# A very short load on a second DMA queue, issued beside the first load, in a 3D average pooling kernel

## The chip, the cores and the metric

One core of one Trainium2 chip. The metric is device time in microseconds (us), as the median of several executions; lower is better.

## The reference, cut to what matters

```python
# x: (8, 32, 32, 32, 32) float32, kernel_size 2
# result: (8, 32, 16, 16, 16) float32
for i in range(16):
    for j in range(16):
        for k in range(16):
            window = x[:, :, 2*i:2*i+2, 2*j:2*j+2, 2*k:2*k+2]
            result[:, :, i, j, k] = np.mean(window, axis=(-3, -2, -1))
```

33.55 MB are read and 4.19 MB written. Every output is the sum of eight inputs times 0.125, so there is little to compute per byte.

## The kernel before: the parts that matter

The 256 pairs of batch and channel make two groups of 128 partitions. The input comes in eight pieces of 4 MB, each of 128 rows of 32 KB, through five buffers; the last two pieces are loaded as two halves each. VectorE adds three times per piece: over d, w and h. An engine (here SP or ScalarE) issues a load or store on its own queue; the 16 DMA engines then move it in packets, one row each for the loads here, and each engine ends its share with a 4-byte completion packet that counts up a semaphore (16 such packets per load in the trace). The transfer has landed when all 16 have counted.

```python
    plan = [
        (0, 0, (32,)), (0, 32, (32,)), (0, 64, (32,)), (0, 96, (32,)),
        (1, 0, (32,)), (1, 32, (32,)), (1, 64, (16, 16)), (1, 96, (16, 16)),
    ]
    # ... pool_unit: three VectorE instructions per part ...
    for t, k0, parts in plan:
        tin = pool_in.tile([P, 32 * KF], F32, tag="tin", name="tin")   # 5 buffers
        # ... per part kb:
            nc.sync.dma_start(out=v, in_=xv[...])                      # SP's queue
        # ... pool_unit on each part
    for queue, t, k0, kb in [(nc.scalar, 1, 0, 2), (nc.sync, 0, 0, 16),
                             (nc.sync, 1, 2, 12), (nc.sync, 1, 14, 2)]:
        queue.dma_start(out=ov[...], in_=obuf[t][...])                 # the four stores
```

The kernel is already tuned at its ends. The program begins with a block in which all engines meet at a barrier; the first load is moved ahead of SP's part of that barrier, so that it is issued with the program's first instruction:

```python
    load = next(i for i in program if isinstance(i, mybir.InstDMACopy))
    # ...
    program.remove(load)
    opening.insert(barrier, load)
```

Of the kernel before, what the change touches and what calls it, by code (L numbers as in the profile page):

```python
# [1 line left out]

# [4 lines left out]

F32 = mybir.dt.float32
KF = 256


@with_exitstack
def pool_rows(
    ctx: ExitStack,
    tc: tile.TileContext,
    x: bass.AP,
    kernel_size: int,
    out: bass.AP,
):
    nc = tc.nc  # L20
    assert kernel_size == 2, "only kernel_size == 2 supported"

    B, C, D, H, W = x.shape
    P = nc.NUM_PARTITIONS
    assert (B * C, D, H, W) == (2 * P, 32, 32, 32)
    add = mybir.AluOpType.add



    xv = x.rearrange("b c d h w -> (b c) (d h w)")  # L30
    ov = out.rearrange("b c d h w -> (b c) (d h w)")




    pool_in = ctx.enter_context(tc.tile_pool(name="pin", bufs=5))
    pool_out = ctx.enter_context(tc.tile_pool(name="pout", bufs=1))
    obuf = [pool_out.tile([P, 16 * KF], F32, name=f"obuf{t}") for t in range(2)]
    dummy = pool_out.tile([P, 1], F32, name="dummy")


    plan = [
        (0, 0, (32,)),
        (0, 32, (32,)),
        (0, 64, (32,)),
        (0, 96, (32,)),
        (1, 0, (32,)),
        (1, 32, (32,)),
        (1, 64, (16, 16)),
        (1, 96, (16, 16)),  # L50
    ]

    def pool_unit(buf, t, k0, kb):

        od = kb // 8
        a = buf.rearrange("p (o dd e) -> p o dd e", o=od, dd=2)
        b = buf[:, :od * 1024]
        nc.vector.tensor_add(  # L58
            out=b.rearrange("p (o e) -> p o e", o=od), in0=a[:, :, 0], in1=a[:, :, 1])
        bv = b.rearrange("p (e ww) -> p e ww", ww=2)  # L60
        c = buf[:, od * 1024:od * 1536]
        nc.vector.tensor_add(out=c, in0=bv[:, :, 0], in1=bv[:, :, 1])  # L62
        cv = c.rearrange("p (j hh k) -> p j hh k", hh=2, k=16)
        o0 = k0 * KF // 8
        nc.vector.tensor_tensor_reduce(  # L65
            out=obuf[t][:, o0:o0 + od * 256].rearrange("p (j k) -> p j k", k=16),
            in0=cv[:, :, 0], in1=cv[:, :, 1],
            scale=0.125, scalar=0.0, op0=add, op1=add, accum_out=dummy[:, :],
        )

    for t, k0, parts in plan:
        tin = pool_in.tile([P, 32 * KF], F32, tag="tin", name="tin")
        views = []
        o = 0
        for kb in parts:
            v = tin[:, o * KF:(o + kb) * KF]
            nc.sync.dma_start(  # L77
                out=v, in_=xv[t * P:(t + 1) * P, (k0 + o) * KF:(k0 + o + kb) * KF])
            views.append((v, k0 + o, kb))
            o += kb  # L80
        for v, k, kb in views:
            pool_unit(v, t, k, kb)



    for queue, t, k0, kb in [
        (nc.scalar, 1, 0, 2),
        (nc.sync, 0, 0, 16),
        (nc.sync, 1, 2, 12),
        (nc.sync, 1, 14, 2),  # L90
    ]:
        queue.dma_start(
            out=ov[t * P:(t + 1) * P, k0 * KF:(k0 + kb) * KF],
            in_=obuf[t][:, k0 * KF:(k0 + kb) * KF],
        )


def kernel(tc: tile.TileContext, x: bass.AP, kernel_size: int, out: bass.AP):
    nc = tc.nc
    pool_rows(tc, x, kernel_size, out)  # L100
    tc.close()
    tc.compile()  # L102
    blocks = nc.main_func.blocks



    opening, program = blocks[0].instructions, blocks[tc.starting_block_idx].instructions
    load = next(i for i in program if isinstance(i, mybir.InstDMACopy))
    assert load.engine == nc.sync.engine
    barrier = next(  # L110
        n for n, i in enumerate(opening)
        if i.engine == load.engine and isinstance(i, mybir.InstDrain))
    program.remove(load)
    opening.insert(barrier, load)




    closing = blocks[-1].instructions
    stores = [  # L120
        i for i in program
        if isinstance(i, mybir.InstDMACopy) and "out_" in i.outs[0].memref]
    kept = [u.id for i in stores for u in i.sync_info.on_update]
    kept = [n for j, n in enumerate(kept) if n not in kept[j + 1:]]
    final = next(
        i for i in closing
        if i.engine == nc.sync.engine and isinstance(i, mybir.InstDrain))
    waits = {w.id: w for w in final.sync_info.on_wait}
    closing[closing.index(final)] = mybir.InstDrain(
        name=final.name, engine=final.engine, ins=[], outs=[], is_reset_sema=False,  # L130
        sync_info=mybir.SyncInfo(
            on_wait=[w for n, w in waits.items() if n not in kept], on_update=[]))


    reset = next(
        n for n, i in enumerate(closing)
        if isinstance(i, mybir.InstDrain) and i.is_reset_sema)
    first, stop = closing[reset].reset_range_start, closing[reset].reset_range_stop
    assert isinstance(closing[reset + 1], mybir.InstISA)
    while len(closing) > reset:  # L140
        closing.pop()
    n = first
    while n < stop:
        m = n
        while m < stop and m not in kept:
            m += 1
        if m > n:
            closing.append(mybir.InstDrain(
                name=nc.get_next_instruction_name(), engine=nc.gpsimd.engine, ins=[], outs=[],
                is_reset_sema=True, reset_range_start=n, reset_range_stop=m))  # L150
            nc.gpsimd.sem_clear(range(n, m))
        n = m + 1
    for n in kept:
        w = waits[n]
        closing.append(mybir.InstEventSemaphore(
            name=nc.get_next_instruction_name(), engine=nc.sync.engine, ins=[], outs=[],
            sync_info=mybir.SyncInfo(
                on_wait=[w],
                on_update=[mybir.SyncUpdate(
                    sync_type="semaphore", id=n, ant_name=w.ant_name,  # L160
                    update_mode="sem-sub-imm", update_value=w.wait_value)])))


# [1 line left out]
_INS = ['x', 'kernel_size']  # L165
_OUTS = [((8, 32, 16, 16, 16), 'float32')]

_NUMBERS = {'kernel_size': 2}


# [26 lines left out]
```

## Time and profile before

| | before |
|---|---|
| median of the three runs | 91.57 us (91.52 to 91.82) |
| profiled execution, first to last instruction | 86.6 us |
| VectorE busy | 64.1 us, 74% |
| DMA | 421 GB/s mean over the span |

From the list of waits (columns: engine, line, who was waited for, total us, times, longest us):

```profile
DVE tin L58 <- DMA tin<-in_x_dram: 20.6, 6, 12.1
```

(DVE is VectorE; in the lines below ACT is ScalarE, and SPq and ACTq are the issuing sides of SP and ScalarE.) VectorE waits for nothing but loads: 12.1 us for the first and 1.7 us for each of the next five. The 12.1 us are the target of the change.

### The profile page before, as it was taken

How to read it: one execution, taken by the hardware profiler on the slowest of the kernel's cores; microseconds unless marked ns; L12 is line 12 of the kernel's file. 1: busy time of each engine (PE TensorE's matmuls, PEld its weight loads, DVE VectorE, ACT ScalarE, POOL GpSimd, SP SyncE). 2: the span in 40 equal slices, each digit the busy share in tenths (PEclk: the TensorE clock that was granted, in tenths of full speed). 3: DMA queues.
4: the chain of work that ended last, by engine and by line, in shares of the span. 5: the costliest groups of instructions: out<-in, count | busy, mean ns of one | idle time of the engine just before them, and what ended most of it. 6: DMA issues, size and time to landing. Idle time of an engine off the chain costs nothing.

```text
span 86.6 us, 91 instructions
## 1 busy us (share of the span) xinstructions
DVE 64.1 (74%) x40; POOL 0.2 (0%) x4
## 2 busy tenths in 40 slices
DVE  0000049993999749992999749992999999999994
POOL 0000000000000000000000000000000000000000
DMA  8889998899979999799988999699999999999999
GB/s 242 379 363 469 485 485 348 379 485 485 469 333 409 485 485 424 318 469 485 485 348 379 485 485 469 288 454 416 405 407 424 407 462 394 462 394 454 394 454 398
DMA packets 1774, 36.48 MB, mean 421 GB/s; under 512 B 192, under 2 KB 192, under 8 KB 320
## 3 DMA queue, kind: packets, MB, share of 16 engines
q1 hardware_dynamic: 1630, 36.22, 98.4%
q10 hardware_dynamic: 144, 0.26, 0.8%
HBM read 33.55 MB, written 4.19 MB: 436 GB/s over the span
## 4 chain that ended last, share of the span: by engine, by line
DMA 83%; DVE 14%; SPq 1%; issue 0%; DVEq 0%
DMA tin<-in_x_dram 83%; DVE tin L58 8%; DVE tin L62 4%; DVE obuf L65 2%; SPq L77 1%; DVE dummy L65 0%; DVEq L102 0%
## 5 line engine op out<-in xcount | busy, mean ns | idle before, releaser
L58 DVE TENSOR_TENSOR tin<-tin 128x4096 f32<-128x4096 f32 (+1 forms) x10 | 35.7, 3570 | 20.7 <-DMA tin<-in_x_dram 20.6
L62 DVE TENSOR_TENSOR tin<-tin 128x2048 f32<-128x2048 f32 (+1 forms) x10 | 18.6, 1865 | 0.3
L65 DVE CUSTOM_DVE_ANT_1 obuf<-tin 128x1024 f32<-128x1024 f32 (+1 forms) x10 | 10.1, 1011 | 0.3
L65 DVE DVE_READ_ACCUMULATOR2_ANT dummy<- 128x1 f32 x10 | 0.8, 82 | 0.0
L178 POOL MEMSET const-uint8-127<- 128x1 uint8 x1 | 0.1, 102 | 0.0
L178 POOL MEMSET const-bfloat16-1.0<- 128x1 bf16 x1 | 0.1, 101 | 0.0
L178 POOL MEMSET const-float32-0.0<- 128x1 f32 x1 | 0.1, 98 | 0.2 <-issue 0.2
L178 POOL MEMSET const-float32-1.0<- 128x1 f32 x1 | 0.1, 98 | 0.0
## 6 DMA issues: line engine op xcount, KB each, us to landing
tin<-in_x_dram SPq DMA_DIRECT2D x6, 4096.0 KB, 35.0
tin<-in_x_dram SPq DMA_DIRECT2D x4, 2048.0 KB, 38.9
out_dram<-obuf SPq DMA_DIRECT2D x1, 2048.0 KB, 36.8
out_dram<-obuf SPq DMA_DIRECT2D x1, 1536.0 KB, 8.8
out_dram<-obuf ACTq DMA_DIRECT2D x1, 256.0 KB, 9.9
out_dram<-obuf SPq DMA_DIRECT2D x1, 256.0 KB, 4.9
```

The costliest lines, as they stand in the source:

```text
L58: nc.vector.tensor_add(out=b.rearrange("p (o e) -> p o e", o=od), in0=a[:, :, 0], in1=a[:, :, 1])
L62: nc.vector.tensor_add(out=c, in0=bv[:, :, 0], in1=bv[:, :, 1])
L65: nc.vector.tensor_tensor_reduce(out=obuf[t][:, o0:o0 + od * 256].rearrange("p (j k) -> p j k", k=16), in0=cv[:, :, 0], in1=cv[:, :, 1], s ...
L77: nc.sync.dma_start(out=v, in_=xv[t * P:(t + 1) * P, (k0 + o) * KF:(k0 + o + kb) * KF])
L178: nc = _bacc.Bacc("TRN2", target_bir_lowering=False, num_devices=1)
```

## The change

The intent, as far as the code tells it: the first transfer of a program may have to wake something on its way, so a tiny one is sent beside it, on the other queue, to wake it first. Nobody reads what it brings.

```diff
     dummy = pool_out.tile([P, 1], F32, name="dummy")
+    first = pool_out.tile([16, 128], F32, name="first")
+    nc.scalar.dma_start(out=first[:, :], in_=xv[:16, :128])
...
-    load = next(i for i in program if isinstance(i, mybir.InstDMACopy))
-    assert load.engine == nc.sync.engine
-    barrier = next(...)
-    program.remove(load)
-    opening.insert(barrier, load)
+    loads = [i for i in program if isinstance(i, mybir.InstDMACopy)][:2]
+    # ... (an assert: the first fills `first`, the second `tin`)
+    for load in loads:
+        assert not load.sync_info.on_wait
+        barrier = next(...)          # the drain of the load's own engine
+        program.remove(load)
+        opening.insert(barrier, load)
```

More of the change, by code (lines that the diff above doesn't have):

```diff
@@ L107 @@
     opening, program = blocks[0].instructions, blocks[tc.starting_block_idx].instructions
-    load = next(i for i in program if isinstance(i, mybir.InstDMACopy))
-    assert load.engine == nc.sync.engine
-    barrier = next(
-        n for n, i in enumerate(opening)
-        if i.engine == load.engine and isinstance(i, mybir.InstDrain))
-    program.remove(load)
-    opening.insert(barrier, load)
+    loads = [i for i in program if isinstance(i, mybir.InstDMACopy)][:2]
+    assert [i.outs[0].bass_ap.tensor.name.split("_")[0] for i in loads] == ["first", "tin"]
+    for load in loads:
+        assert not load.sync_info.on_wait
+        barrier = next(
+            n for n, i in enumerate(opening)
+            if i.engine == load.engine and isinstance(i, mybir.InstDrain))
+        program.remove(load)
+        opening.insert(barrier, load)
     closing = blocks[-1].instructions
```

## The prediction

> **What bounds the kernel now.** I read the page from the top. First the engines, the DMA row in 40 slices, the queues and the memory traffic:
>
> ```profile
> DVE 64.1 (74%) x40; POOL 0.2 (0%) x4
> ...
> DMA  8889998899979999799988999699999999999999
> ...
> q1 hardware_dynamic: 1630, 36.22, 98.4%
> q10 hardware_dynamic: 144, 0.26, 0.8%
> HBM read 33.55 MB, written 4.19 MB: 436 GB/s over the span
> ```
>
> VectorE, the only computing engine, is busy 74% of the span; the 16 DMA engines are close to 90% or more in nearly every slice, and the two queues' packets add up to 99.2% of 16 engines' time. q10 carries 144 packets and 0.26 MB, which is exactly the one 256 KB store that the source gives to ScalarE (128 rows and 16 completions), so q10 is ScalarE's queue and q1 is SP's. Today q10 is first used when that store is issued, at 59.01 us.
>
> Then the chain that ended last, which says the same in time:
>
> ```profile
> DMA 83%; DVE 14%; SPq 1%; issue 0%; DVEq 0%
> ```
>
> Last, the timeline of the first additions, each of which starts as soon as a 4 MB load has landed (columns: start, duration, engine, line, what, and in brackets the idle time before and who ended it):
>
> ```profile
> 0.00 2.66 SPq L77 DMA_DIRECT2D tin<-in_x_dram  x5
> ...
> 12.12 4.42 DVE L58 TENSOR_TENSOR tin<-tin 128x4096 f32<-128x4096 f32 x1 [12.12 <-DMA tin<-in_x_dram]
> ...
> 21.81 4.43 DVE L58 TENSOR_TENSOR tin<-tin 128x4096 f32<-128x4096 f32 x1 [1.68 <-DMA tin<-in_x_dram]
> ...
> 31.53 4.43 DVE L58 TENSOR_TENSOR tin<-tin 128x4096 f32<-128x4096 f32 x1 [1.70 <-DMA tin<-in_x_dram]
> ```
>
> VectorE idles 1.7 us before each of these, so the stream sets the pace: one 4 MB load per 9.7 us (21.81 - 12.12 = 9.69, 31.53 - 21.81 = 9.72), 4.194 MB / 9.7 us = 432 GB/s. The first load needs 12.12 us instead of 9.7, so **opening the stream costs 2.4 us** in all. That is the only place where a load beside the first one can earn anything. It splits further. In the trace's packet records the first packet of the first load begins 1.01 us after its issue; the 16 engines begin theirs between 1.01 and 1.72 us; and those first 16 packets of 32 KB take 1.35 to 2.15 us, mean about 1.8, where the later ones take 1.21 to 1.24. Whatever their start, they all end between 2.8 and 3.3 us. So some 0.6 us of the opening is a slow first packet, about 1.0 us is issue to first byte, and the rest is spread between engines and completion.
>
> At the other end, the last store's completions land at 90.37 us in the trace, after 85.49, where it was issued behind a 1.5 MB store. The measured 91.57 us thus follows the end of the DMA stream, not VectorE, whose last instruction ends at 85.5. Start of the stream, bytes over rate, end of the stream: these three make the time.
>
> **What the Trainium skill says.** "DMA: Bandwidth & Descriptors", section "Issuing engines are not separate DMA queues": transfers from different issuers run on the same 16 DMA engines and interleave; a second issuer saves only the sequencer's issue time. The trace agrees so far that q1 and q10 together fill 99.2% and no more. Same page, section "Why a DMA increments its semaphore by 16 and not by 1": the number of engines is the largest k up to 16 that divides the slowest dimension of both sides. 16 rows give 16 engines with one row each; the trace before has 16 completions per load of 128 rows, in line with it, but no 16-row load. "Perfetto Trace Analysis", section "DMA Instruction — HWDGE (DVE, Sync)": the block that generates descriptors is shared and locked by one sequencer at a time, and the recorded issue includes waiting for that lock. No two issues coincide in the trace before, so it can't show this; single issues last 327 to 527 ns. No page that I found says that a first DMA warms anything for the next one.
>
> **The change part by part.** It removes nothing. It adds a load of 16 rows x 128 floats = 8 KB into a buffer that nobody reads, in front of the opening barrier on ScalarE's queue, and with it a tile of 512 B per partition.
>
> 1. Bytes. One 512 B packet and one 4-byte completion per engine. The steady rate is 432/16 = 27 GB/s per engine, so 512 B is 19 ns; the completion packets are recorded with 9 ns. For scale, a 2048 B packet of a store takes 84 ns, a quarter of which is 21. The sum is about 0.03 us, wholly on the path because the engines are full until the end. **+0.03 us.**
>
> 2. Issue. ScalarE spends some 0.35 to 0.4 us on it (its one store issue took 0.38). It has nothing else to do until 59.01 us, so that costs nothing by itself. If the generator is locked by it just ahead of SP, SP's first load starts late by at most that issue, 0.4 us. In the trace the first record of SP (its load) stands at 0.00 and ScalarE's first (a drain) at 0.13 us, so SP will probably come first and ScalarE will wait. I give the bad order one chance in four: **+0.1 us** on average at the most.
>
> 3. Opening barrier. ScalarE's drain moves behind its issue, from 0.13 to about 0.5 to 0.9 us. SP's own drain ends at 0.56 and the barrier opens at 0.71, so it may open up to 0.4 us later and SP's second load is issued at about 1.2 instead of 0.79 us. That is hidden: each engine still has 8 packets of the first load to move, until about 11.7 us.
>
> 4. Opening of the stream. If the 512 B packets pay part of the first-packet delay ahead of the large ones, the stream begins up to 0.6 us earlier, and since it then runs full all that comes off the end. But both loads leave at the same time, so the small one can't be far ahead. I give a third of the possible: **-0.2 us.**
>
> 5. Semaphores and buffers. One more transfer shifts the semaphores that loads and stores use by one place, since these are given out in turn. The load that reuses the small one's semaphore is issued in the middle of the run, long after 3 us, when the small one has landed. The closing handles the same four stores. **0.**
>
> Sum: 91.57 + 0.03 + 0.1 - 0.2 = 91.5 us.
>
> **The rivals.** *Hidden anyway*: the small load is lost in the stream, +0.03 us, 91.6. For it: nothing in the chain waits on ScalarE, and 8 KB is 0.02% of 37.75 MB. *It opens the path*: ScalarE's packets take the 0.6 us of the first fetch and the large ones then take 1.23 us at once; 91.0. For it: the 16 first packets end together whatever their start, as if a common delay held them. Against: the simultaneous issue. *It steals the generator*: SP's first issue is delayed, all starts shift by 0.3 to 0.4 us, 91.9 to 92.0. For it: two issues at the same instant on a shared block; against: SP's head start of 0.13 us. *VectorE becomes the bound*: not possible here, it gains 1.7 us of slack per 4 MB and gets no work.
>
> **Range and chances.** The rivals span 91.0 to 92.0; the three runs before spread from 91.52 to 91.82, so 0.15 us of noise lies on either side. I take 91.5, and 91.1 to 91.9 for 8 in 10. Two per cent is 1.8 us, three quarters of the whole opening cost of 2.4 us, and no step comes near it: within 2% gets 0.98, the sides 0.01 each.
>
> **What would show it.** Right, if q10 has 32 more packets, the first addition starts within 0.4 us of 12.12, the spacing stays at 9.7 us, and the last completion moves by as much as the first addition does. Step 2 is shown by SP's first issue lasting 0.7 us or its first packet beginning after 1.3; step 4 by first packets of 32 KB that take under 1.5 us; step 3 by a second issue near 1.2 us and engines that nonetheless show no gap at the end of the first load. Wrong, if a slow engine is thrown out of step for the rest of the run, if the opening delay is much more than one packet's and the small load takes it over, or if the stores' end changes.

## More of the kernel before

The groups of runs ran on different chips of the machine, so each group has its own runs of the kernel before.

## The result, and the profile after

| | before | after |
|---|---|---|
| median | 91.68 us (91.52 to 91.82, 6 runs) | 91.89 us (91.66 to 91.95, 6 runs) |
| ratio, 95% interval | | 1.0018 (1.0002 to 1.0034) |
| profiled span | 86.6 us | 86.4 us |

Ratios here and below are the mean time of one kernel's fast runs over that of the other's of the same rounds, so not quite the ratio of the medians.

First the DMA row, the queues and the chain of the kernel after:

```profile
DMA  8989998999979999799979999798999999999999
...
q1 hardware_dynamic: 1629, 36.21, 98.6%
q10 hardware_dynamic: 176, 0.27, 0.8%
HBM read 33.56 MB, written 4.19 MB: 437 GB/s over the span
...
DMA 83%; DVE 14%; SPq 1%; issue 0%; DVEq 0%
```

q10, ScalarE's queue, has 176 packets in place of 144: 16 of 512 B and 16 completions more. The rest is as it was, down to the shares of the chain. Then the timeline's opening:

```profile
0.00 40.35 SPq L79 DMA_DIRECT2D tin<-in_x_dram  x10
0.12 0.38 ACTq L41 DMA_DIRECT2D first<-in_x_dram  x1
...
12.08 4.42 DVE L60 TENSOR_TENSOR tin<-tin 128x4096 f32<-128x4096 f32 x1 [12.08 <-DMA tin<-in_x_dram]
...
21.79 4.42 DVE L60 TENSOR_TENSOR tin<-tin 128x4096 f32<-128x4096 f32 x1 [1.70 <-DMA tin<-in_x_dram]
```

ScalarE issues the small load 0.12 us after SP has begun with the large one. The first piece is there at 12.08 us, against 12.12 before: the opening is unchanged. Last, the list of DMA issues (name, queue, count, KB, us from issue to landing):

```profile
first<-in_x_dram ACTq DMA_DIRECT2D x1, 8.0 KB, 4.7
```

8 KB took 4.7 us. The packet records of the trace (queue, size, start and duration of every packet; not the engine) tell why: the 16 first packets of 32 KB are all under way, side by side, by 1.60 us, and each 512 B packet starts only as one of them ends, between 2.63 and 3.20 us. Its completion comes one more 32 KB packet later. The load that was to open the way went second.

So two questions are left. Is the 0.17 us of the first comparison real? And would the idea work if the small load did go first?

### The profile page after: what moved, and what is told of

It is laid out like the page before. It is cut to its first block, busy times and chain, and to the rows that moved or that the text cites. A ratio compares the mean times of both kernels' runs of the same rounds, so it can differ in the third digit from the quotient of the medians.

```text
span 86.4 us, 91 instructions
## 1 busy us (share of the span) xinstructions
DVE 64.1 (74%) x40; POOL 0.2 (0%) x4
## 4 chain that ended last, share of the span: by engine, by line
DMA 83%; DVE 14%; SPq 1%; issue 0%; DVEq 0%
DMA tin<-in_x_dram 83%; DVE tin L60 8%; DVE tin L64 4%; DVE obuf L67 2%; SPq L79 1%; DVE dummy L67 0%; DVEq L104 0%
```

## The experiments

The theories: **A**, the small load costs what its packets take in a full stream, some hundredths of a us, and there is nothing to warm. **B**, it costs 0.17 us through something fixed (the later barrier, the shifted semaphores). **C**, warming is real, but the small load came too late for it. Against all of them stands chance.

### 1. The kernel before as its own rival, and the changed kernel again (e1_null, e2_again, e11_again2)

No edit: e1_null is the kernel before, the others are the changed kernel.

> The kernel before, unchanged, run as if it were a new one. It tells how far a ratio of 1.0018 can come from the measuring alone. If the 0.17 us of the change are real: ratio 1.000, interval within 0.9990 to 1.0010, and clearly below the repeat of the changed kernel. If they are the measuring's own (order of runs, another build): ratio 1.001 to 1.002 as for the changed kernel.

> The changed kernel once more with more rounds. Real cost: ratio 1.0010 to 1.0030 again with an interval above 1. Chance: interval across 1.000. The opening, by the trace: first 32 KB packets begin at 1.03 to 1.6 us and last 1.8 us, small packets come only after them (2.6 to 3.2 us).

> The changed kernel a third time. From the trace its cost is one 512 B packet (33 to 40 ns) and one completion (9 ns) per engine, 0.05 us or a ratio of 1.0005, less than the spread of the kernel before (91.53 to 92.28). If the first comparison's 1.0018 was chance: 0.9995 to 1.0015, interval across 1. If there is a real 0.17 us: 1.0015 to 1.0025, interval above 1.

| | median, us | ratio to before, 95% |
|---|---|---|
| e1_null | 91.80 | 1.0001 (0.9980 to 1.0023) |
| first comparison | 91.89 | 1.0018 (1.0002 to 1.0034) |
| e2_again | 91.88 | 1.0007 (0.9986 to 1.0028) |
| e11_again2 | 91.89 | 1.0006 (0.9993 to 1.0020) |

The changed kernel's median hardly moves: 91.88 to 91.89 three times. It is the kernel before that moved: medians of 91.68, 91.81 and 91.84 in these comparisons, single runs from 91.52 to 92.28. The intervals of the two repeats cross 1, so 0.17 us is not confirmed: they estimate 0.06 us. But they reach up to 0.26 and 0.18 us, and the kernel before against itself is known to no better than 0.2 us, so 0.17 us is not excluded either. The three comparisons of the changed kernel, weighted by their intervals, give 1.0010 (1.0001 to 1.0020), some 0.1 us. More than that the times can't say; for so small a difference the argument goes by the traces. In the traces of both repeats the small packets again come after the first large ones, from 2.72 and 2.68 us on.

### 2. More packets in the same load (e3_rows128)

```diff
-    first = pool_out.tile([16, 128], F32, name="first")
-    nc.scalar.dma_start(out=first[:, :], in_=xv[:16, :128])
+    first = pool_out.tile([P, 128], F32, name="first")
+    nc.scalar.dma_start(out=first[:, :], in_=xv[:P, :128])
```

> The same small load with 128 rows in place of 16: eight packets of 512 B per engine in place of one, still one issue and one completion per engine. Theory A (packets on the full engines cost what their records last, about 40 ns each): 7 more packets are 0.28 us, time 0.25 to 0.35 us above the changed kernel, so about 92.15. Theory B (the cost of the change is fixed: the issue, the barrier, the semaphores): equal to the changed kernel within 0.1 us. Theory C (there is no cost): equal to before.

Median 91.95 us, ratio 1.0015 (0.9993 to 1.0038): 0.07 us above e2_again, less than the 0.25 expected, and not clear. In the timeline the first addition starts later:

```profile
12.36 4.43 DVE L60 TENSOR_TENSOR tin<-tin 128x4096 f32<-128x4096 f32 x1 [12.36 <-DMA tin<-in_x_dram]
```

In the three traces of the changed kernel (the first, e2_again, e11_again2) the same addition starts at 12.08, 12.03 and 12.24 us, so 0.12 to 0.33 us earlier. That has the sign that theory A gives and room for its size, but one trace can't tell it from this scatter; section 5 does. The packet records show the first 512 B packet of each engine lasting 28 to 42 ns and the others mostly 27, one after each 32 KB packet: a step of 1.24 us. By the tenth and last load nothing of the lateness is left to see (it lands at 81.37 us, against 81.13, 81.28 and 81.40); this comes back below.

### 3. The small load after the barrier (e4_inside)

```diff
-    loads = [i for i in program if isinstance(i, mybir.InstDMACopy)][:2]
+    loads = [i for i in program if isinstance(i, mybir.InstDMACopy)][1:2]   # the large one alone
```

> The small load stays on ScalarE's queue but is issued after the opening barrier, not ahead of it; the first load alone is ahead of it as before. Theory B, barrier (it opened 0.14 us later in the trace, 0.844 in place of 0.708 us): the barrier is back at 0.71 us and the time back at the level of before. Theory A, packets: same bytes and packets in the full stream, so the same time as the changed kernel. Theory D (semaphores shifted, closing): as the changed kernel, too.

Median 91.88 us, ratio 1.0008 (0.9984 to 1.0032), as e2_again. In the changed kernel SP leaves the barrier at 0.84 us and issues its second large load at 0.93; in e4_inside that issue is back at 0.79, where it was before the change, and it bought nothing. The interval of the times is too wide to show that alone, but the traces do: the second load lands at 21.77 us with the late barrier, at 21.76 in e4_inside and at 21.79 in the kernel before. The barrier's delay is hidden behind the first load's packets. Theory B in its barrier form falls; its shifted semaphores have no run of their own.

### 4. The small load truly first (e5_sp_first, e6_wait)

e5 puts it on SP's queue, one issue ahead of the large load; e6 leaves it on ScalarE's and lets SP wait until it has landed.

```diff
# e5_sp_first
-    nc.scalar.dma_start(out=first[:, :], in_=xv[:16, :128])
+    nc.sync.dma_start(out=first[:, :], in_=xv[:16, :128])
# e6_wait: in the opening, ahead of the large load
+    done = loads[0].sync_info.on_update[0]
     # ...
+    opening.insert(opening.index(loads[1]), mybir.InstEventSemaphore(
+        # ... engine=nc.sync.engine, on_wait: id=done.id, "sem-ge-imm", wait_value=16
+        ))
```

> The small load issued on SP's queue just ahead of the first large one, so that its 512 B packets must run first. Warming theory (the extra 0.6 us of the first 32 KB packets is paid once, by whichever packet comes first): the first 32 KB packets last 1.2 to 1.3 us instead of 1.8, and the first chunk lands no later than 0.3 us after that of before, although its issue is 0.4 us later: time 91.6 to 91.9. Latency theory (each queue start has that delay, or the large load pays its own): first 32 KB packets still 1.7 to 1.8 us, everything 0.4 us later: 92.1 to 92.3.

> The changed kernel, but SP waits until the small load has landed before it issues the first large one (a wait on a constant, in the opening). By then everything a first transfer can warm is warm. The small load alone should land 2 to 2.5 us after its issue, so the time grows by about that, to 93.8 to 94.4 us, in any theory. What tells them apart is the first 32 KB packets, counted from SP's issue: warming: they last 1.2 to 1.3 us, and the first chunk lands 11.4 us after the issue; latency: 1.8 us and 12.0 us after the issue, as in the kernel before.

e5: 92.30 us, ratio 1.0046 (1.0026 to 1.0067). e6: 93.69 us, ratio 1.0192 (1.0170 to 1.0215). The timeline of e5, then of e6:

```profile
0.00 0.38 SPq L41 DMA_DIRECT2D first<-in_x_dram  x1
...
0.44 2.63 SPq L79 DMA_DIRECT2D tin<-in_x_dram  x5
12.51 4.42 DVE L60 TENSOR_TENSOR tin<-tin 128x4096 f32<-128x4096 f32 x1 [12.51 <-DMA tin<-in_x_dram]
```

```profile
0.00 0.38 ACTq L41 DMA_DIRECT2D first<-in_x_dram  x1
...
1.63 2.61 SPq L79 DMA_DIRECT2D tin<-in_x_dram  x5
13.71 4.43 DVE L60 TENSOR_TENSOR tin<-tin 128x4096 f32<-128x4096 f32 x1 [13.71 <-DMA tin<-in_x_dram]
```

From e6's list of DMA issues (KB, us from issue to landing) comes the landing of the small load:

```profile
first<-in_x_dram ACTq DMA_DIRECT2D x1, 8.0 KB, 1.6
```

Count from the issue of the large load: 12.51 - 0.44 = 12.07 us and 13.71 - 1.63 = 12.08 us, against 12.12 in the kernel before. The first packets say the same (from the packet records; times from the issue of the first large load):

| | first packet begins | mean duration of the first 16 | their mean end |
|---|---|---|---|
| before | 1.01 us | 1.80 us | 3.05 us |
| after | 1.03 us | 1.82 us | 2.99 us |
| e5_sp_first | 1.03 us | 1.77 us | 3.00 us |
| e6_wait | 1.01 us | 1.82 us | 2.96 us |

Warming by this load had its chance and did nothing: in e6 the small load had landed before the large one was issued, and the large one opened as slowly as ever. Theory C falls for a load of 16 rows of 512 B; a larger one, or one issued much earlier, was not tried as a warm-up. Each microsecond that the large load starts later is paid in full (e5: 0.44 us later, 0.42 us by the ratio; e6: 1.63 us later, 1.76 by the ratio). e6 cost less than I had expected because an 8 KB load by itself lands 1.6 us after its issue, not 2 to 2.5.

### 5. A larger dose: bytes and packets (e7_bytes512k, e8_packets64)

Both bring 512 KB, e7 in 8 packets of 4 KB per engine, e8 in 64 of 512 B.

```diff
# e7
+    first = pool_out.tile([P, 1024], F32, name="first")
+    nc.scalar.dma_start(out=first[:, :], in_=xv[:P, :1024])
# e8: the same tile, from every second block of 128 floats
+    nc.scalar.dma_start(
+        out=first.rearrange("p (a c) -> p a c", c=128),
+        in_=xv[:P, :2048].rearrange("p (a b c) -> p a b c", b=2, c=128)[:, :, 0, :])
```

> The small load grown to 128 rows of 4 KB, 512 KB in all, 8 packets of 4 KB per engine. If every byte ahead in the stream is paid at the end (the stream bounds the kernel): 0.524 MB / 432 GB/s = 1.2 us more, so 92.9 to 93.1 us. If transfers hide in some slack of the DMA engines: less than 0.5 us.

> The same 512 KB in packets of 512 B: 64 per engine. If only bytes count: the same time as with packets of 4 KB, within 0.2 us. If a packet of 512 B costs what its record lasts, 27 to 40 ns: 64 x 27 = 1.7 us to 2.6 us, so 93.5 to 94.3 us, and a single one, as in the change, costs 0.03 to 0.04 us and its completion 0.01.

e7: 92.95 us, ratio 1.0115 (1.0091 to 1.0139), so 1.06 us for the 1.2 expected: bytes in this stream are paid for; there is no slack of a us to hide them in.

e8: 95.96 us, ratio 1.0445 (1.0421 to 1.0469): 4.1 us, far above both expectations. The timeline of e8:

```profile
22.17 4.42 DVE L62 TENSOR_TENSOR tin<-tin 128x4096 f32<-128x4096 f32 x1 [1.96 <-DMA tin<-in_x_dram]
32.14 4.43 DVE L62 TENSOR_TENSOR tin<-tin 128x4096 f32<-128x4096 f32 x1 [1.95 <-DMA tin<-in_x_dram]
...
62.12 4.43 DVE L62 TENSOR_TENSOR tin<-tin 128x4096 f32<-128x4096 f32 x1 [2.02 <-DMA tin<-in_x_dram]
62.37 1.85 SPq L81 DMA_DIRECT2D tin<-in_x_dram  x4
...
69.52 2.29 DVE L62 TENSOR_TENSOR tin<-tin 128x2048 f32<-128x2048 f32 x1 [0.64 <-DMA tin<-in_x_dram]
```

A 4 MB load now takes 9.97 us, not 9.71. The packet records count 144 small packets in the 10 us from 20 to 30 us, 9 per engine: as many as a load's 8 large packets and its completion packet together. So 0.26 us are **29 ns for each of 9** (the expectation of the next section still reckons with 8, and 33 ns). By 62 us that makes 1.5 us. The rest is another thing, and the waits of SP's queue name it:

```profile
SPq L81 <- DMA first<-in_x_dram: 41.8, 1, 41.8
```

The list of DMA issues has the landing:

```profile
first<-in_x_dram ACTq DMA_DIRECT2D x1, 512.0 KB, 62.2
```

SP waited 41.8 us *for the small load*. Semaphores of transfers are given out in turn, and the seventh large load gets the one that the small load had, so it may not be issued until that has landed. With its 512 B packets alternating with those of SP's queue, the small load took until 62.3 us: the six loads ahead offer only some 50 turns per engine for its 64 packets, and the last 13 per engine went after 61 us, as SP's queue ran out. By then the last 4 MB on SP's queue had landed too (62.1 us), the queue was empty, and the next piece was there only at 69.5 us, 7.4 us after the last one, where e2_again needs 5.4 for a piece of that size (60.6 to 65.9 us): 2.0 us of the 4.1. The last 0.6 us were lost later: between 80 and 85 us the packets of 16 KB, which take 0.61 us before and after, take up to 1.34 us. Summed and divided by the 16 engines, that is 1.12 us more than usual, against 0.40 us in a weaker phase of this kind in e2_again. The other runs have such phases too (next section); what sets them off is not shown.

The refilling of the empty queue also answers a question that e5 and e6 left. The load that SP issues at 62.37 us is far from the program's first, and yet its first 16 packets (16 KB) begin 0.96 us after the issue and last 1.12 us on average, where those of the middle of the run take 0.61: a slow opening of +0.51 us, like the +0.6 us at the program's start.

### 6. Half that dose (e9_packets32, e12_packets32b)

```diff
# against e8
-    first = pool_out.tile([P, 1024], F32, name="first")
+    first = pool_out.tile([P, 512], F32, name="first")
-        in_=xv[:P, :2048].rearrange(...)
+        in_=xv[:P, :1024].rearrange(...)
```

> As the run with 64 packets of 512 B per engine, but 32. In that run the small load landed only at 62.3 us (its packets alternate one by one with the 32 KB ones), the seventh large load waits for its semaphore, and the queue of SP ran empty; the loads before it took 9.97 us instead of 9.71, 33 ns per packet of 512 B. Theory: 64 x 33 ns = 2.1 us of its 4.1 us are packets, 2.0 us are the empty queue. With 32 packets the small load lands at about 42 us, the seventh large load is issued then and not at 30, but the loads before it last until 60 us: no empty queue, cost 32 x 33 ns = 1.1 us, time 92.8 to 93.1. Rival: all 4.1 us are the packets' (64 ns each): 93.8 to 94.0.

> The run with 32 packets of 512 B per engine once more. There the fourth large load landed 0.93 us later than in the kernel before (29 ns per packet), but the end came only 0.49 us later; the stretch from the sixth landing to the ninth, in which nothing of the small load is left, took 20.2 us in place of 20.5 to 20.85. If that stretch was short by chance: now 20.5 or more and a time of 92.6 to 92.9. If a later start of that stretch makes it shorter each time: 20.2 again and 92.2 to 92.4.

e9: 92.30 us, ratio 1.0053 (1.0036 to 1.0069). e12: 92.35 us, ratio 1.0062 (1.0049 to 1.0074). The small load landed at 40.9 us, SP issued its seventh load right then, and the queue never ran empty. That part came out as expected. The time did not: 0.49 and 0.57 us for the expected 1.1. With 29 ns per packet 0.9 us were to be expected, so some 0.4 us are missing. The landings show where they went (us; stretch is the difference between the 6th and the 10th, which is the last; the expectation above calls it the ninth by mistake):

| | 4th load | 6th | 10th | stretch 6th to 10th | last store |
|---|---|---|---|---|---|
| before | 41.22 | 60.65 | 81.15 | 20.51 | 90.37 |
| e1_null | 41.16 | 60.59 | 81.16 | 20.57 | 90.38 |
| after | 41.19 | 60.63 | 81.13 | 20.50 | 90.27 |
| e2_again | 41.15 | 60.58 | 81.28 | 20.70 | 90.43 |
| e3_rows128 | 41.48 | 60.90 | 81.37 | 20.46 | 90.50 |
| e4_inside | 41.19 | 60.61 | 81.46 | 20.85 | 90.60 |
| e9_packets32 | 42.10 | 61.52 | 81.71 | 20.19 | 90.83 |
| e12_packets32b | 42.06 | 61.49 | 81.80 | 20.31 | 90.95 |

Up to the 6th landing the dose costs 0.9 us in both runs (29 ns per packet); then a stretch in which none of the small packets are left is shorter than in any other run. In the eleven runs without a dose of 32 or 64 this stretch varies between 20.46 and 20.85 us (e5, e6, e7, e10 and e11 lie in it too). In all of them the packets of 16 KB are slowed for some us, between 60 and 66 us, between 78 and 81, or in both places: the longest take 0.81 us in place of 0.61 in the kernel before and 1.24 in e1_null. What the large packets of the stretch last beyond their usual time, per engine, is 0.22 to 0.68 us in those runs, 0.13 in e9 and 0.23 in e12; without that the stretch takes 20.0 to 20.2 us in each of these thirteen runs. So the dose is paid, and the slow phases after it were weak. A variation of that size is larger than anything that the change itself does. Why they were weak after the dose of 32, twice, is **left open**; a later start alone does not do it, as e6's stretch starts later still (62.6 us) and takes 20.46.

### 7. What the slow first packets are (e10_split8)

```diff
-        (0, 0, (32,)),
+        (0, 0, (8, 24)),
```

> The kernel before with its first 4 MB load cut in two: 128 rows of 8 KB, then 24 KB. No small load. It asks what the 0.6 us of the first 16 packets are. A fixed delay of the first packet whatever its size: 8 KB packets last 0.9 us. Slowness in proportion (16 engines starting together on rows 128 KB apart): they last 0.45 us, half more than 0.3. The first addition (on 1 MB) can start near 4.5 us in place of 12.1. The time is that of before within 0.3 us in both cases, as the stream's bytes are the same and VectorE is not on the path until its end; if the stream fills earlier, up to 0.3 us less.

91.93 us, ratio 1.0011 (0.9996 to 1.0025): nothing gained. The first addition starts at 4.78 us, but that on the rest of the piece at 12.05, as before:

```profile
4.78 1.22 DVE L58 TENSOR_TENSOR tin<-tin 128x1024 f32<-128x1024 f32 x1 [4.78 <-DMA tin<-in_x_dram]
...
12.05 3.36 DVE L58 TENSOR_TENSOR tin<-tin 128x3072 f32<-128x3072 f32 x1 [4.86 <-DMA tin<-in_x_dram]
```

The packets of 8 KB fit neither expectation: the 16 that began first last 0.61 us on average, the next 16 0.36, and those after the first 48 0.31. So it is neither one fixed delay per first packet nor slowness in proportion for a whole packet of 32 KB: all packets are slow until about 2 us after the issue. Together with e5, e6 and the refilled queue of e8 this says that the slow phase belongs to the start of a large load on 16 idle engines, not to the first transfer of the program. What happens in it is not shown by these runs.

## Why the prediction was right, and which of its steps were not

91.5 us with a range of 91.1 to 91.9 and "within 2%" at 0.98: the result of 91.89 is inside, by 0.01 us. That "within 2%" held is no luck, as no step came near 2%; that the range held, by so little, is luck. Its steps:

1. **Bytes, +0.03 us.** Right in kind. The packet costs 29 ns in the full stream (e8), not the 19 ns that its bytes would; with 9 ns for the completion about 0.04 us. The measured ratio of the repeats, 1.0006 and 1.0007, is 0.06 us and not clear of zero.
2. **Issue, +0.1 us for the chance that ScalarE goes first.** That chance did not come up: SP was first by 0.12 us in all three traces of the changed kernel, and its issue lasted 381 to 383 ns, against 382. What a delayed first issue would cost is measured by e5: about 0.42 us for 0.44 us of delay.
3. **Barrier, hidden.** Right: 0.14 us later in the trace (0.84 in place of 0.71 us, where up to 0.4 was allowed), and e4, which takes the delay away, is no faster.
4. **Opening, -0.2 us. This step failed.** The prediction gave the small load "a third of the possible" of the 0.6 us in the first packets. It got nothing: the first 32 KB packets still last 1.82 us, against 1.80, where the prediction named under 1.5 as the sign of this step. There are two reasons, which the runs separate: it went second (its packets come after the first 32 KB packets), and had it gone first it would have changed nothing (e5, e6).
5. **Semaphores, 0.** Right for 8 KB, which land at 4.8 us. But the dependence is real: in e8 it emptied the queue and cost 2.0 us.

The sum without step 4 and with the good order of step 2 is 91.57 + 0.04 = 91.6. Of the other 0.3 us, 0.1 is the base: all six runs of that comparison have a median of 91.68, and the kernel before had 91.81 to 91.88 in the later ones. The other 0.2 us are the difference of the first comparison, which the repeats put at 0.06. The allowance of 0.15 us on either side was taken from three runs and was too small.

Of the rivals, "hidden anyway" won. "It opens the path" is refuted for this kernel and this small load (e6), and "it steals the generator" did not happen, as SP came first.

## What to carry to other kernels

Before warming something up, make the warm-up come first by force, with a wait if need be, and measure the thing itself: one such run (e6) settled here what the change as written could not. What lengthened this stream, full from start to end, was a later start (e5, e6), more bytes (e7) and more packets (e8); a useless load is paid for by its packets. A difference of 0.2% wants the old kernel run as its own rival before it gets a cause; and a transfer that nobody waits for can still hold up a later one that was given its semaphore.

## What the Trainium skill lacked or had wrong

- "DMA: Bandwidth & Descriptors", section "Latency and other measured facts", gives about 600 ns to the first byte for loads issued from SP or ScalarE. Here the first packet record of the first large load begins 1.00 to 1.03 us after the start of its issue, in all runs. From the end of the issue, 0.38 us later, it is 0.63 us in the kernel before, which would agree; the page lacks from where it counts.
- "Perfetto Trace Analysis", section "DMA Instruction — HWDGE (DVE, Sync)", lets one sequencer at a time use the descriptor generator and counts the wait for it into the issue. Here SP's first issue (0.00 to 0.38 us) and ScalarE's (0.12 to 0.50) overlapped by 0.26 us, and neither was longer than alone: 383 and 381 ns, against 382 in the kernel before and 381 in e6_wait. In e4_inside the two issues even began 5 ns apart and lasted 381 (ScalarE) and 332 ns (SP's second, 332 in the kernel before too). SP's third issue did grow, from 424 ns to 752 in the changed kernel and 484 to 646 in the other runs with a small load in that place; no run separates the cause.
- "DMA: Bandwidth & Descriptors", section "Queues, rings and completion order", says that an engine takes turns between queues packet by packet. This agrees, and it lacks the consequence: a queue of short packets beside a queue of 32 KB ones gets one turn per packet of the other, here 9 in 10 us, so that 64 packets of 512 B per engine landed 62.2 us after their issue, and the last 13 of them only because the other queue had run out (e8_packets64).
- No page that I found says that the first transfer of a program needs warming, and the runs agree: the first large load opens in the same 12.1 us with or without one before it (e5_sp_first, e6_wait), and a load on an emptied queue at 62.4 us opens slowly too (e8_packets64).
- No page that I found warns that semaphores given out in turn tie a late small transfer to a later load: 41.8 us of waiting on SP's queue in e8_packets64.
